# Rotary embedding over split heads on one core: the final wait for the stores moves from SyncE to GpSimd

## The chip, the core and the metric

The kernel runs on one core of a Trainium2 chip. The core has five engines, each with its own instruction stream: TensorE (PE), VectorE (DVE), ScalarE (ACT), GpSimd (POOL) and SyncE (SP); they meet only through semaphores. Bulk transfers are done by 16 DMA engines, which an engine starts by issuing a DMA instruction into its queue. The metric is device time in microseconds, lower is better. The kernel as it stands takes 161.19 us, the median of three runs (161.04 to 161.2).

## The reference: what is computed

`x` has 16 batches of 512 positions of 1024 float32 numbers, which are 16 heads of 64. Each head is cut into two halves of 32, and the two are rotated by a table of cosines and sines that depends on the position alone:

```python
x = x.reshape(batch, seq, num_heads, head_dim)
x1, x2 = x[..., :half_dim], x[..., half_dim:]
cos, sin = cos[None, :, None, :], sin[None, :, None, :]
rotated = np.concatenate([x1 * cos - x2 * sin, x1 * sin + x2 * cos], axis=-1)
```

The input and the output have 33.55 MB each, and every input element is read once and every output element is written once.

## The kernel before, in words

A **unit** is a 128 x 1024 tile: 128 partitions, one row of 16 heads in each. There are 64 units. Positions are spread over the partitions, four neighbouring rows per partition for a single batch (4 units, 2 MB, one DMA each way) or eight for a pair of batches (8 units, 4 MB, one DMA each way). The first two and the last two batches are handled as singles, the twelve between them as six pairs: ten loads and ten stores in all. The tiles live in `x_sb`, a ring of 40 units, and the result is written over the input in place.

The work of one unit is a product with the cosines, a product of the swapped halves with the signed sines, and their sum:

- POOL computes most of the sine products into `t2_sb` (`on_gpsimd`, line 263), in groups of one or two units. Its program begins with a memset and an `affine_select` that make the identity matrix, and it ends with the last product.
- DVE computes the cosine product into PSUM (line 302), a few of the sine products (line 295), and for two thirds of the units the sum (line 313).
- For the other third, PE adds `t2_sb` onto the cosine product in PSUM by a matmul with the identity (line 225), and ACT copies the sum back to `x_sb` (line 192).

ACT also issues every load (line 154) and the loads of the two tables (line 175). The six loads that fit into the ring are issued at the start; the last four wait until the store that frees their part of the ring has landed (semaphores `sem_out[k]`, of which there are `EARLY` = 3).

SP issues the stores and does nothing else (`on_sync`, lines 157 to 163). For each tile it waits until the last unit of the tile has been added up (`wait_added`, the waits at line 138), and issues the store (line 162). The first stores raise `sem_out[k]`, all later ones raise `sem_rest`; the six of `sem_rest` raise it by 16 each, to 96. The last instruction of SP's program is a wait for that 96 (line 163), so SP's program ends only when every store of these six has landed; the earlier stores are waited for by ACT ahead of the late loads. PE, ACT, POOL and DVE have no such last wait: their programs end with their last piece of arithmetic.

Of the kernel before, what the change touches and what calls it, by code (L numbers as in the profile page):

```python
# [6 lines left out]
def bass_split_heads_rope_kernel(  # L7
# [22 lines left out]
    R2 = 2 * R1  # L30
# [15 lines left out]
    NU = len(rows)  # L46
    EARLY = (NU - RING) // R2
# [24 lines left out]
    with ExitStack() as stack:  # L72
# [13 lines left out]
        sem_rest = stack.enter_context(nc.semaphore("rest"))  # L86
# [27 lines left out]
        def in_dram(single, pairs, t):  # L114
            b, n = tiles[t]
            return single[b] if n == R1 else pairs[:, b:b + 2, :]

        def in_sbuf(t):
            b, n = tiles[t]
            k = b * R1 % RING  # L120
            return x_sb[:, k:k + n].rearrange("p n h t d -> p (n h t d)")

        def where(u):
            t, r = rows[u]
            return t, r, u % RING
# [7 lines left out]
        def wait_added(eng, u):  # L133

            if n_pe[u]:
                eng.wait_ge(sem_a, n_pe[u])
            if n_comb[u]:
                eng.wait_ge(sem_v, n_comb[u])

        def wait_t2_free(eng, u):  # L140

            if u >= NT2:
                v = u - NT2
                if PE2[v]:
                    eng.wait_ge(sem_e, n_pe[v])
                else:
                    eng.wait_ge(sem_v, n_comb[v])

        def stores_of(k):

            return sum(b * R1 // R2 == k for b, _ in tiles)
# [4 lines left out]
        def on_sync(sp):  # L156
            for u in range(NU):
                t, r, k = where(u)
                if r == tiles[t][1] - 1:
                    wait_added(sp, u)  # L160
                    k = u // R2
                    sp.dma_start(in_dram(o1, o2, t), in_sbuf(t)).then_inc(sem_out[k] if k < EARLY else sem_rest, 16)
            sp.wait_ge(sem_rest, 16 * sum(stores_of(k) for k in range(EARLY, NU // R2)))

        def on_scalar(ae):
            later = {}
# [68 lines left out]
        def on_gpsimd(pl):  # L235
            pl.memset(ident[:], 1.0).then_inc(sem_i, 1)  # L236
            pl.wait_ge(sem_i, 1)
            pl.affine_select(  # L238
                out=ident[:],
                in_=ident[:],  # L240
                compare_op=mybir.AluOpType.is_equal,
                fill=0.0,
                base=0,
                pattern=[[-1, P]],
                channel_multiplier=1,
            ).then_inc(sem_i, 1)
            for u in range(NU):
                if V2[u] or (G2[u] and u % 2 == 1):
                    continue
                t, r, k = where(u)  # L250
                n = 2 if G2[u] else 1
                if (t, r) == (0, 0):
                    pl.wait_ge(sem_s, 1)
                if (t, r) == (2, 0):
                    pl.wait_ge(sem_s, 2)
                if r == 0:
                    pl.wait_ge(sem_in[t], 16)
                if n == 2 and u + 1 >= NT2:
                    pl.wait_ge(sem_m, u + 2 - NT2 + NT1)  # L259
                elif n == 1:  # L260
                    wait_t2_free(pl, u)
                table = (s1_sb if tiles[t][1] == R1 else s2_sb)[:, r:r + n]
                pl.tensor_tensor(  # L263
                    t2_sb[:, u % NT2:u % NT2 + n],
                    x_sb[:, k:k + n, :, ::-1, :],
                    table[:, :, None, :, :].broadcast_to([P, n, H, 2, HALF]),
                    mult,
                ).then_inc(sem_p, 1)

        def on_vector(ve):  # L270
            ve.memset(zero[:], 0.0).then_inc(sem_z, 1)  # L271
# [48 lines left out]
            for u in range(NU + LEAD):  # L320
                if u < NU:
                    mul(u)
                if u >= LEAD and not PE2[u - LEAD]:
                    comb(u - LEAD)

        on_sync(nc.sync)
        on_scalar(nc.scalar)
        on_gpsimd(nc.gpsimd)
        on_tensor(nc.tensor)
        on_vector(nc.vector)  # L330
# [33 lines left out]
```

## Time and profile before

| what | value |
|---|---|
| median of three runs | 161.19 us (161.04 to 161.2) |
| time of the profiled execution | 161.04 us |
| its span, first to last instruction of the program | 159.6 us |
| time outside the span | 1.4 us |
| busy: POOL, DVE, PE, ACT | 131.7, 129.6, 64.4, 24.3 us |
| moved by DMA | 67.25 MB, 421 GB/s over the span |
| last store: issued, landed | 151.9 us, 159.6 us |

The span begins with the first instruction of the program on any engine and ends with the last one. Instants in the text are microseconds from the span's start. An engine is called busy while it computes; semaphore waits and DMA issues are not counted. The letter q behind an engine's name means the part of it that issues instructions, its sequencer: SPq is where SP's waits and DMA issues are listed. Beside its instructions, the trace records when each semaphore was changed, also by instructions around the program that have no line of the kernel.

### The profile page before, as it was taken

The numbers are of one execution on the slowest core, as the hardware profiler recorded it, in microseconds if no ns is written. First come the engines' busy times: TensorE is split into PE (matmuls) and PEld (weight loads), VectorE is DVE, ScalarE is ACT, GpSimd is POOL, SyncE is SP. The second block draws the span as 40 slices with busy tenths as digits, with TensorE's granted clock in tenths as the row PEclk, the third lists the DMA queues.
The fourth block names the chain that finished last, engine by engine and source line by source line (L and its number), as shares of the span: only waits on it lengthen the run. The fifth ranks groups of instructions, "written<-read, shape, count | busy, mean of one in ns | idle before, by whom it ended". The sixth has DMA issues, their size and how long they took to land.

```text
span 159.6 us, 499 instructions
## 1 busy us (share of the span) xinstructions
PE 64.4 (40%) x94; PEld 22.2 (14%) x94; DVE 129.6 (81%) x117; ACT 24.3 (15%) x27; POOL 131.7 (82%) x41
## 2 busy tenths in 40 slices
PE   6050017076408870789067400575058506900000
PEld 1020011021102220222021100211021102300000
DVE  0069947999999989998999629999999999556900
ACT  0420002004300250023102040023202310220000
POOL 1069999999999999999999798992999999089400
PEclk9999999759985589557759985589957995585555
DMA  5999999999999999999999999999999999999997
GB/s 144 396 466 472 394 411 431 448 476 402 394 448 406 495 419 402 476 435 402 443 435 435 394 476 435 402 460 394 427 456 448 443 394 423 472 419 435 386 456 300
DMA packets 3169, 67.25 MB, mean 421 GB/s; under 512 B 352, under 2 KB 608, under 8 KB 608
## 3 DMA queue, kind: packets, MB, share of 16 engines
q10 hardware_dynamic: 1728, 33.69, 49.8%
q1 hardware_dynamic: 1440, 33.56, 48.9%
q14 instruction: 1, 0.01, 0.0%
HBM read 33.69 MB, written 33.55 MB: 421 GB/s over the span
## 4 chain that ended last, share of the span: by engine, by line
DMA 61%; DVE 17%; POOL 5%; PE 5%; issue 4%; ACTq 1%; ACT 1%; DVEq 0%; POOLq 0%; SPq 0%
DMA x_sb<-in_x_dram 43%; DMA out_dram<-x_sb 18%; DVE t_ps L302 8%; DVE x_sb L313 7%; POOL t_sb L263 5%; PE t_ps L225 5%; DVE t_sb L295 2%; ACT x_sb L192 1%; ACTq L154 1%; ACTq L175 1%; DVE tab_ps L280 0%; DVEq L312 0%; DVE tab_ps L281 0%; DVEq L299 0%; POOLq L259 0%
## 5 line engine op out<-in xcount | busy, mean ns | idle before, releaser
L263 POOL TENSOR_TENSOR t_sb<-x_sb,s_sb 128x2048 f32<-128x2048 f32 (+1 forms) x35 | 131.0, 3784 | 17.1 <-DMA x_sb<-in_x_dram 8.3
L225 PE MATMUL t_ps<-t_sb,ident 128*128 128x512 f32 x84 | 59.6, 857 | 69.1 <-DVE t_ps L302 56.7
L302 DVE TENSOR_TENSOR t_ps<-x_sb,pair_ps 128x1024 f32<-128x1024 f32 x48 | 57.5, 1221 | 5.2 <-ACT x_sb L192 5.2
L313 DVE TENSOR_TENSOR x_sb<-t_ps,t_sb 128x1024 f32<-128x1024 f32 x43 | 52.2, 1216 | 5.9 <-POOL t_sb L263 5.9
L192 ACT ACTIVATE x_sb<-t_ps 128x1024 f32<-128x1024 f32 x21 | 21.4, 1024 | 107.6 <-PE t_ps L225 99.9
L225 PEld LDWEIGHTS t_ps<-t_sb,ident 128*128 128x128 f32 x84 | 20.3, 267 | 108.2 <-DVE t_ps L302 78.7
L302 DVE TENSOR_TENSOR t_ps<-x_sb,tab_ps 128x1024 f32<-128x1024 f32 x16 | 19.2, 1222 | 2.6 <-DMA x_sb<-in_x_dram 2.5
L295 DVE TENSOR_TENSOR t_sb<-x_sb,tab_ps 128x1024 f32<-128x1024 f32 x6 | 7.3, 1209 | 0.0
L273 DVE COPY tab_ps<-stage 128x128 f32<-128x128 f32 x1 | 0.3, 296 | 7.6 <-DMA stage<-in_cos_dram 7.6
L209 PE MATMUL pair_ps<-stage,pick 128*128 128x256 f32 x4 | 2.0, 667 | 5.1 <-DMA stage<-in_sin_dram 5.1
L202 PE MATMUL t_ps<-zero 128*128 128x512 bf16 x6 | 2.7, 629 | 1.3 <-DVE zero L271 1.3
L178 ACT ACT_TABLE_LOAD x1 | 1.3, 1283 | 5.5 <-issue 5.5
L209 PEld LDWEIGHTS pair_ps<-stage,pick 128*128 128x128 f32 x4 | 1.2, 324 | 6.1 <-issue 6.0
L202 PEld LDWEIGHTS t_ps<-zero 128*128 128x128 bf16 x6 | 0.7, 136 | 2.4 <-DVE zero L271 1.2
L271 DVE MEMSET zero<- 128x256 uint32 x1 | 0.3, 272 | 0.9 <-PEq L346 0.9
L187 ACT ACTIVATE s_sb<-pair_ps 128x256 f32<-128x256 f32 x1 | 0.4, 384 | 1.7 <-PE pair_ps L209 1.7
L183 ACT ACTIVATE s_sb<-stage 128x128 f32<-128x128 f32 x1 | 0.3, 310 | 1.8 <-DMA stage<-in_sin_dram 1.8
L236 POOL MEMSET ident<- 128x128 f32 x1 | 0.2, 205 | 0.3 <-POOLq L346 0.3
L178 ACT ACTIVATE pick<-ident 128x256 f32<-128x256 f32 x1 | 0.4, 416 | 0.0
L188 ACT ACTIVATE s_sb<-pair_ps 128x256 f32<-128x256 f32 x1 | 0.4, 377 | 0.0
L238 POOL TENSOR_SCALAR_AFFINE_SELECT ident<-ident 128x128 f32<-128x128 f32 x1 | 0.3, 295 | 0.1
L346 POOL MEMSET const-float32-0.0<- 128x1 f32 x1 | 0.1, 99 | 0.3 <-issue 0.3
(6 smaller groups left out, 1.0 us busy)
## 6 DMA issues: line engine op xcount, KB each, us to landing
x_sb<-in_x_dram ACTq DMA_DIRECT2D x6, 4096.0 KB, 38.7
out_dram<-x_sb SPq DMA_DIRECT2D x6, 4096.0 KB, 25.3
x_sb<-in_x_dram ACTq DMA_DIRECT2D x4, 2048.0 KB, 22.7
out_dram<-x_sb SPq DMA_DIRECT2D x4, 2048.0 KB, 16.1
stage<-in_cos_dram ACTq DMA_DIRECT2D x1, 64.0 KB, 7.5
stage<-in_sin_dram ACTq DMA_DIRECT2D x1, 64.0 KB, 7.2
```

The source lines that it names most:

```text
L154: eng.dma_start(in_sbuf(t), in_dram(x1, x2, t)).then_inc(sem_in[t], 16)
L175: ae.dma_start(stage[:, i, :], table.rearrange("(s r) d -> s (r d)", r=R1)).then_inc(sem, 16)
L178: ae.activation(pick[:], ident[:].rearrange("q (s k) -> q k s", k=2)[:, :, :, None].broadcast_to([P, 2, P // 2, 2]), COPY).then_inc(sem_g, 1)
L187: ae.activation(s2[:, :, :, 0, :], pair_ps[:, :, 1, :, :], COPY, scale=-1.0)
L192: ae.activation(xs[:, u % RING, :], t1_ps[:, u % NT1, :], COPY).then_inc(sem_a, 1)
L202: pe.matmul(t1_ps[:, k, b * BANK:(b + 1) * BANK], zero[:, 0:P], zero[:], start=True, stop=True).then_inc(sem_w, 1)
L209: pe.matmul(pair_ps[:, k].rearrange("p c r d -> p (c r d)"), pick[:, k].rearrange("q s b -> q (s b)"), stage[:].rearrange("q c f -> q (c f)"),
L225: ins = pe.matmul(t1_ps[:, u % NT1, b * BANK:(b + 1) * BANK], ident[:], t2[:, b * BANK:(b + 1) * BANK], start=False, stop=True, skip_group ...
L263: pl.tensor_tensor(t2_sb[:, u % NT2:u % NT2 + n], x_sb[:, k:k + n, :, ::-1, :], table[:, :, None, :, :].broadcast_to([P, n, H, 2, HALF]), ...
L295: ve.tensor_tensor(t2_sb[:, u % NT2, :, :, :], swapped(k), over_heads(v_ps), mult)
L302: ve.tensor_tensor(t1_ps[:, u % NT1, :].rearrange("p (h d) -> p h d", d=HALF), x_sb[:, k, :, :, :].rearrange("p h t d -> p (h t) d"), c_of ...
L313: ve.tensor_tensor(xs[:, k, :], t1_ps[:, u % NT1, :], t2_sb[:, u % NT2, :, :, :].rearrange("p h t d -> p (h t d)"), add,).then_inc(sem_v, 1)
```

## The change

The last wait of SP's program is removed, and the same wait, for the same semaphore and the same value, is put behind the loop at the end of POOL's program. Nothing else is touched: the number of instructions, the DMAs and their order are the same.

```diff
@@ on_sync
                     sp.dma_start(in_dram(o1, o2, t), in_sbuf(t)).then_inc(sem_out[k] if k < EARLY else sem_rest, 16)
-            sp.wait_ge(sem_rest, 16 * sum(stores_of(k) for k in range(EARLY, NU // R2)))
@@ on_gpsimd
                     mult,
                 ).then_inc(sem_p, 1)
+            pl.wait_ge(sem_rest, 16 * sum(stores_of(k) for k in range(EARLY, NU // R2)))
```

## The prediction, made before the changed kernel was run

> **What bounds the kernel now.** I read the page first: the slices of the span, then the chain that ended last.
>
> ```profile
> span 159.6 us, 499 instructions
> ...
> DMA  5999999999999999999999999999999999999997
> ...
> DMA 61%; DVE 17%; POOL 5%; PE 5%; issue 4%; ACTq 1%; ACT 1%; DVEq 0%; POOLq 0%; SPq 0%
> ```
>
> The DMA engines are at 90% or more in 38 of 40 slices, and 61% of the chain is transfers. The kernel is bound by moving 67.25 MB; no engine's arithmetic can be what the change touches. Next, the end of the span: SP's waits, its last instruction, and the timeline of SP and POOL after 140 us.
>
> ```profile
> SPq L163 <- DMA out_dram<-x_sb: 7.4, 1, 7.4
> ```
> ```profile
> L163 SPq EVENT_SEMAPHORE  x1: 17/17/17, 159.6 to 159.6; - x1
> ```
> ```profile
> 140.88 11.33 SPq L162 DMA_DIRECT2D out_dram<-x_sb  x2
> ```
> ```profile
> 140.32 9.12 POOL L263 TENSOR_TENSOR t_sb<-x_sb,s_sb 128x2048 f32<-128x2048 f32 x3 [4.32 <-DMA x_sb<-in_x_dram]
> ```
>
> SP issues its last store by 140.88 + 11.33 = 152.2 us and waits 7.4 us for it; this wait is the last instruction of the whole program. POOL's last product ends at 140.32 + 9.12 = 149.44, so POOL stands still for 10.2 us before the same landing. The landing doesn't depend on who waits: whatever the change does, it does in the 1.4 us between the span (159.6) and the time (161.04).
>
> What happens there has no row in the views, but the trace's record of semaphore updates goes on past the span. One semaphore, number 2, belongs to none of the program's instructions. It is raised nine times in a burst, twice ahead of the first instruction and twice at the end (us from the span's start):
>
> ```
> ahead 1: -7.857 -3.493 -2.871 -2.827 -2.804 -2.691 -2.653 -2.619 -2.569
> ahead 2: -0.371 -0.336 -0.298 -0.254 -0.231 -0.120 -0.081 -0.047 -0.001
> end 1:  139.968 140.968 149.973 151.952 159.739 159.783 159.822 159.856 159.904
> end 2:  160.868 160.902 160.940 160.984 161.008 161.106 161.144 161.178 161.225
> ```
>
> The first five of "end 1" fit the ends of the five engines, read from the last update that each made: PE 139.812, ACT 140.868, POOL 149.450, DVE 151.813, and SP's wait that ends at 159.629. So I read it as a barrier that walks a fixed chain, PE, ACT, POOL, DVE, SP, and then back, DVE, POOL, ACT, PE; an engine raises the count when its predecessor has. Between the two end barriers about 240 other semaphores change once each, from 159.864 to 160.472, in five blocks of neighbouring numbers; the last block (3 to 53, ending 160.472) starts after PE's release at 159.904. Then "end 2" starts, with PE. So from PE's release everything follows in a fixed 161.225 - 159.904 = 1.32 us.
>
> **The change, step by step.**
>
> *Removed: SP's wait.* SP's program ends at 152.2. Its end then lies under the store's 7.4 us and costs nothing; SP stands in the chain behind DVE, which arrives at 151.952, and would have to wait for POOL anyway. What leaves the path is SP's arrival, 159.739 - 159.629 = 0.110 us, and the way back from SP, 159.904 - 159.739 = 0.165 us. Together 0.275 us.
>
> *Added: POOL's wait.* Nothing in the program is queued behind it: it stands after POOL's last product, no DMA is issued by POOL, and no engine waits for POOL's wait. What is behind it is POOL's place in the barrier, and DVE and SP, which follow in the chain, now wait for POOL. The instruction itself is the same (17 ns on SPq; the program's opening wait on POOLq is 17 ns too):
>
> ```profile
> L346 POOLq EVENT_SEMAPHORE  x2: 17/17/17, 0.6 to 0.7; - x2
> ...
> L346 SPq DRAIN  x1: 7/7/7, 0.0 to 0.0; - x1
> ...
> L346 POOLq DRAIN  x1: 187/187/187, 0.4 to 0.4; - x1
> ```
>
> How quickly POOL notices a landing: its product at 140.32 starts 0.068 us after the last update of that load (140.252), DVE's at 140.28 0.028 us after. I take 0 more than SP and keep 0.05 for the range.
>
> *The way through the barrier with POOL last.* DVE and SP must still go up, then four steps back. The other bursts show just that, from the third update to the ninth: 161.225 - 160.940 = 0.285, -0.001 + 0.298 = 0.297, -2.569 + 2.871 = 0.302 us; in "ahead 1" POOL really was the late one, by 0.62 us. Mean 0.295 against SP's 0.165: **+0.13 us**. The steps aren't alike: SP to DVE takes 0.044 where DVE had long been waiting, and 0.098 to 0.113 where DVE itself had just gone up, as it would here.
>
> The Trainium skill, "Runtime: NRT & Kernel Launch", section on the preamble and postamble, describes such a pass over five engines with 44 ns a step and about 355 ns for eight. "End 2" takes 0.357 us for its eight steps, so the total agrees; by equal steps, POOL last would have six steps to go where SP has four, +0.09 us, an estimate. That would put the sum 0.04 lower than by the rows.
>
> *POOL's own arrival.* This is the disputed term. From an engine's last update to its raise of semaphore 2: PE 0.156, ACT 0.100, DVE 0.139, SP 0.110, but POOL 149.973 - 149.450 = **0.523 us**. Today that is hidden: DVE is 2 us later, SP 10 us. After the change it stands in the open. Below, it can't be much less than the other engines' 0.100. Above, all 0.523 stays, and something may be added: POOL's sequencer was free from about 147.1, when its last product started, so closing instructions of POOL that ran under that 2.35 us product would come into the open too. The nearest rows for such are POOL's opening ones (MOVE 35 ns, INC_SWDGE_SEM 27 ns), so I bound it at 0.2.
>
> Which part is tied to finishing arithmetic? In the opening, POOL's DRAIN reports at 0.625 (update of semaphore 96), 0.12 after the last memset (0.40 + 0.10), where idle engines' DRAINs take 7 to 10 ns. So I let 0 to 0.12 of the 0.523 fall away when POOL has been idle for 10 us, and 0.40 to 0.52 stay. I take 0.47, which is 0.36 more than SP's 0.110.
>
> *Sum:* 0.13 + 0.36 = **+0.49 us** on the profiled execution: 161.04 + 0.49 = 161.53. The bounds are 0.13 - 0.01 = +0.12 and 0.13 + 0.41 + 0.2 + 0.05 = +0.79. The profiled execution was the lowest of the three runs, 0.15 below the median; the runs differ by their transfers, not by this end, so against the median I predict 161.19 + 0.49 = **161.68 us**. This kernel's measurement can tell 0.2% or 0.32 us from no change, so "slower" begins at 161.51.
>
> **The rivals.**
>
> *A: POOL's 0.523 us is only the tail of its product.* Then a POOL that has idled arrives like the others (0.100 to 0.156), and only the barrier's +0.13 is left: 161.32, not slower by what can be told. For it: POOL's spans are the least exact of the page, and only one arrival of POOL after arithmetic is in the trace. Against it: consecutive products follow without a gap (three in 9.12 us: 4.50 + 2.35 + 2.35 and a little overlap), so a finished product leaves no 0.4 us behind, and the DRAIN row allows 0.12. It decides if POOL arrives less than 0.30 us after its wait ends.
>
> *B: the time doesn't contain the barrier.* If the 1.4 us lay ahead of the first instruction, the end would be the last wait on either engine: 161.19, at most 0.05 more. Against it: the last update is 161.225 - 159.629 = 1.60 us after SP's wait, and the 1.41 us fit inside that but for 0.19.
>
> *C: SP's ending is what costs.* SP's stores are its queue's; if SP's closing has to settle that queue, it would now be done under the 7.4 us, and the barrier might close sooner. The most that leaves the path is the 0.275 us above, and POOL must arrive and return in no time: 160.92. SP's arrival of 0.110 beside ACT's 0.100 shows nothing heavy.
>
> *D: POOL's hidden closing is long.* The 2.35 us product could cover more than my 0.2; then 161.98 and up, without a row for it.
>
> **How the numbers follow.** Forecast (+0.33 to +0.79): 0.60. D: 0.06. A: 0.24. B: 0.07. C: 0.03. The forecast and D are slower, 0.66; A and B within 0.2%, 0.31; C, to which I leave the chance of a real gain, faster, 0.03. The range goes from 161.2, which takes in A and half of B, to 162.0, the upper bound 161.19 + 0.79; outside are C, most of D and half of B, with run-to-run differences of 0.1 about 0.15 in all.
>
> **What would show it.** In the changed profile the span should stay within the transfers' own differences of 159.6, its last instruction an EVENT_SEMAPHORE on POOLq in place of SPq, after an idle stretch of about 10 us on POOL. The loads, stores and products should show the same durations. The third update of semaphore 2 should be the late one, about 0.47 us after POOL's wait (A: 0.10 to 0.16); DVE and SP should follow in 0.044 and 0.024, and the ninth update 0.295 after the third. From there to the end it should be 1.32 us as now. I'm wrong if the time outside the span stays at 1.4 us (A would make it 1.5, the forecast 1.9), or if a store's issue or landing moved by more than the runs differ, for which I see no reason.

## The result, and the profile after

The changed kernel takes 162.0 us, the median of eight runs (161.69 to 162.9), against 161.19 us of the kernel before (eight runs, 161.04 to 161.58). The ratio is 1.0046, with a 95% interval of 1.0028 to 1.0065: slower by about half a per cent. The profiled execution took 161.95 us with a span of 160.0 us. In the experiments below, a few executions, of the kernel before too, took 3 to 7 us longer than the rest, and all ratios, medians and counts leave these out.

The page's head, slices and chain of the changed kernel:

```profile
span 160.0 us, 499 instructions
...
DMA  5999999999999999999999999999999999999997
...
DMA 61%; DVE 17%; POOL 5%; PE 5%; issue 4%; ACTq 1%; ACT 1%; DVEq 0%; POOLq 0%; SPq 0%
```

This is the old picture: nothing in the body has another bound. What changed is the last instruction. First POOL's wait (the row of line 268), then SP's last stores in the timeline, then POOL's last products:

```profile
L268 POOLq EVENT_SEMAPHORE  x1: 17/17/17, 160.0 to 160.0; - x1
```
```profile
142.32 10.18 SPq L162 DMA_DIRECT2D out_dram<-x_sb  x2
```
```profile
140.60 9.12 POOL L262 TENSOR_TENSOR t_sb<-x_sb,s_sb 128x2048 f32<-128x2048 f32 x3 [4.54 <-DMA x_sb<-in_x_dram]
```

SP's program ends at 142.32 + 10.18 = 152.5 us by this row. POOL is done with its arithmetic at 149.72, and its wait of 17 ns is now the last instruction of the program. The product's line numbers are one lower, since a line went away above them.

The updates of semaphore 2, the barrier around the program, at the end of the two profiled executions (us from the span's start; the span ends at 159.629 before and at 159.976 after):

```
before, end 1: 139.968 140.968 149.973 151.952 159.739 159.783 159.822 159.856 159.904
before, end 2: 160.868 160.902 160.940 160.984 161.008 161.106 161.144 161.178 161.225
after,  end 1: 141.409 142.406 160.513 160.556 160.580 160.676 160.715 160.749 160.796
after,  end 2: 161.761 161.796 161.834 161.877 161.901 162.000 162.038 162.072 162.119
```

Before, the fifth raise (SP) is the late one; after, it is the third (POOL), and DVE and SP follow it at once. **POOL's arrival** is 160.513 - 159.976 = 0.537 us after its wait ends, where SP's was 0.110. **The way** from the late raise to PE's release, the ninth raise, is 0.283 us, where SP's was 0.165. From PE's release to the last raise are 1.323 us, before 1.321. So the time outside the span went from 161.04 - 159.63 = 1.41 us to 161.95 - 159.98 = 1.97 us, +0.56, and 0.43 + 0.12 of it are these two terms.

The rest of the difference of the medians, 0.81 - 0.56 = 0.25 us, is in the span: in all eight runs the time exceeds the span by 1.94 to 2.00 us, so what they have beyond that is span. It isn't explained by either term and is followed up below.

### The profile page after: what moved, and what is told of

It is laid out like the page before. It is cut to its first block, busy times and chain, and to the rows that moved or that the text cites. A ratio compares the mean times of both kernels' runs of the same rounds, so it can differ in the third digit from the quotient of the medians.

```text
span 160.0 us, 499 instructions
## 1 busy us (share of the span) xinstructions
PE 69.5 (43%) x94; PEld 24.0 (15%) x94; DVE 129.7 (81%) x117; ACT 24.3 (15%) x27; POOL 131.6 (82%) x41
## 4 chain that ended last, share of the span: by engine, by line
DMA 61%; DVE 17%; POOL 5%; PE 5%; issue 4%; ACTq 1%; ACT 1%; DVEq 0%; POOLq 0%; SPq 0%
DMA x_sb<-in_x_dram 42%; DMA out_dram<-x_sb 18%; DVE t_ps L302 8%; DVE x_sb L313 7%; POOL t_sb L262 5%; PE t_ps L224 5%; DVE t_sb L295 2%; ACT x_sb L191 1%; ACTq L154 1%; ACTq L174 1%; DVE tab_ps L280 0%; DVEq L312 0%; DVE tab_ps L281 0%; DVEq L299 0%; POOLq L258 0%
## 5 line engine op out<-in xcount | busy, mean ns | idle before, releaser
L224 PE MATMUL t_ps<-t_sb,ident 128*128 128x512 f32 x84 | 64.7, 929 | 65.3 <-DVE t_ps L302 53.0
L224 PEld LDWEIGHTS t_ps<-t_sb,ident 128*128 128x128 f32 x84 | 22.1, 291 | 107.8 <-DVE t_ps L302 76.6
```

The lines of the kernel that those rows point to most:

```text
L224: ins = pe.matmul(t1_ps[:, u % NT1, b * BANK:(b + 1) * BANK], ident[:], t2[:, b * BANK:(b + 1) * BANK], start=False, stop=True, skip_group ...
```

## The experiments

All ratios are to the kernel before, run on the same chip in turn. The table gathers what the profiled executions show; the columns "arrival" (from the end of the last wait or instruction to the raise of semaphore 2 by that engine) and "way" (from there to the ninth raise) are read from the record of updates.

| kernel | last to arrive | time | span | outside | arrival | way | ratio (95% interval) |
|---|---|---|---|---|---|---|---|
| again_before | SP | 161.49 | 160.07 | 1.42 | 0.110 | 0.163 | 1.0002 (0.9993 to 1.0011) |
| sp_twice | SP | 161.26 | 159.85 | 1.41 | 0.110 | 0.165 | 1.0007 (0.9998 to 1.0016) |
| wait_dve | DVE | 161.39 | 159.86 | 1.53 | 0.146 | 0.242 | 1.0015 (1.0001 to 1.0029) |
| wait_act | ACT | 161.60 | 160.01 | 1.59 | 0.119 | 0.324 | 1.0001 (0.9982 to 1.0021) |
| wait_pe | PE | 162.81 | 159.74 | 3.07 | 0.187 | 0.355 | 1.0062 (1.0034 to 1.0091) |
| again_after | POOL | 162.32 | 160.35 | 1.97 | 0.537 | 0.286 | 1.0062 (1.0045 to 1.008) |
| third_after | POOL | 161.74 | 159.78 | 1.97 | 0.537 | 0.286 | 1.0053 (1.004 to 1.0066) |
| wait_both | POOL | 161.75 | 159.80 | 1.96 | 0.537 | 0.285 | 1.0032 (1.0022 to 1.0043) |
| wait_both_2 | POOL | 161.78 | 159.81 | 1.97 | 0.537 | 0.286 | 1.0032 (1.002 to 1.0045) |
| after_sp_pad | POOL | 162.10 | 160.13 | 1.97 | 0.538 | 0.282 | 1.0046 (1.0033 to 1.0059) |
| pool_memset | POOL | 162.09 | 160.15 | 1.94 | 0.517 | 0.285 | 1.005 (1.0038 to 1.0062) |
| sp_155 | POOL | 161.72 | 159.76 | 1.97 | 0.538 | 0.286 | 1.0049 (1.0031 to 1.0066) |

**The theory and its rivals.** Theory 1 is the prediction's: each engine has its own closing, and its place in the chain sets how many steps are left. Rivals: the place is nothing and POOL's closing is all; or it isn't POOL at all but SP, whose program now ends while its stores are under way.

**The two kernels again, as a control and for the spans.** No edit.

> The kernel before, unchanged, as a control. Theory 1 (the added time is all outside the span: 0.53 us of POOL's own closing plus 0.28 us of way through the chain, against SP's 0.11 and 0.165): time minus span 1.41 us, ratio 1.000. It also gives the spans of before, of which only one, 159.6, was shown; the rival to be told apart is that the change lengthens the span too, by about 0.25 us (half of what was measured over the forecast).

> The changed kernel, unchanged, on the same chip as the control. Theory 1: time minus span 1.97 us, and a median span within 0.1 us of the control's, so a ratio of 1.0034 (0.56 of 161.2). Rival (the span is lengthened by the change as well): median span 0.25 us or more above the control's, ratio 1.005.

The control is the kernel before to 1.0002, and its 1.42 us outside the span is the old 1.41. The changed kernel has 1.97 again, and a ratio whose interval lies above 1.0034: the span is longer as well (median 160.3 us, the control's 159.9). The head of the control's page, then that of the changed kernel's:

```profile
span 160.1 us, 499 instructions
```
```profile
span 160.3 us, 499 instructions
```

**Both engines wait.** It tells POOL's part from SP's.

```diff
 # on top of the changed kernel, at the end of on_sync
+            sp.wait_ge(sem_rest, 16 * sum(stores_of(k) for k in range(EARLY, NU // R2)))
```

> POOL's wait as in the changed kernel, and SP keeps its own. Theory 1 (POOL's place and POOL's closing): as the changed kernel, time minus span 1.97 us, third update of semaphore 2 about 0.53 us after the wait, ratio 1.0034. Rival (what costs is that SP's program ends while its stores are under way): as before, time minus span 1.41 us, ratio 1.000; and if that is what lengthened the span, the span is as the control's.

```profile
SPq L163 <- DMA out_dram<-x_sb: 7.4, 1, 7.4
```
```profile
L269 POOLq EVENT_SEMAPHORE  x1: 17/17/17, 159.8 to 159.8; - x1
```

SP waits its 7.4 us as before the change, and the end still costs 1.96 us outside the span: the cost outside is POOL's and not that of SP's early end. But the ratio is 1.0032, as these 0.55 us alone would make it: the longer span isn't there (median 159.8 us).

**The wait on DVE, on ACT, on PE.** SP's wait is removed and put behind the last instruction of the other engine's program:

```diff
+            ve.wait_ge(sem_rest, ...)     # wait_dve, end of on_vector
+            ae.wait_ge(sem_rest, ...)     # wait_act, end of on_scalar
+            pe.wait_ge(sem_rest, ...)     # wait_pe,  end of on_tensor
```

> The wait stands at the end of DVE's program, and nowhere else. Theory 1: DVE arrives 0.12 to 0.14 us after its wait, then 0.024 up to SP and 0.098 + 0.038 + 0.034 + 0.047 back: 0.36 to 0.38 us from the end of the wait to PE's release against SP's 0.275, so time minus span 1.50 to 1.52 us, ratio 1.0006. Rival (any engine but SP costs as much as POOL, since SP has gone ahead): 1.97 us, ratio 1.0034.

> The wait stands at the end of ACT's program alone, second in the chain. Theory 1 (own closing plus way): ACT arrives 0.10 to 0.13 us after its wait, and from ACT's raise to the end of the chain are 0.32 us; 0.43 us against SP's 0.275, time minus span 1.56 to 1.58 us, ratio 1.001. Rival (the place in the chain is nothing, an engine's closing is all): 1.41 us, ratio 1.000.

> The wait stands at the end of PE's program alone, at the head of the chain. Theory 1: PE arrives about 0.16 us after its wait and the whole chain follows, 0.357 us: 0.51 us to PE's release against SP's 0.275, time minus span 1.65 us, ratio 1.0015 from the end alone. Rival (POOL's closing is all that costs, the place in the chain is nothing): 1.41 to 1.46 us. SP ends early here too: if that lengthens the span, the median is 0.25 us more.

The last instruction of each, in the order DVE, ACT, PE:

```profile
L324 DVEq EVENT_SEMAPHORE  x1: 21/21/21, 159.8 to 159.8; - x1
```
```profile
L196 ACTq EVENT_SEMAPHORE  x1: 17/17/17, 160.0 to 160.0; - x1
```
```profile
L233 PEldq EVENT_SEMAPHORE  x1: 51/51/51, 159.7 to 159.7; - x1
```

The raises of semaphore 2 around the release, in the same order:

```
wait_dve, end 1: 141.145 142.144 150.179 160.002 160.025 160.123 160.161 160.197 160.244
wait_act, end 1: 140.602 160.131 160.169 160.213 160.237 160.334 160.372 160.408 160.455
wait_pe,  end 1: 159.922 159.956 159.994 160.038 160.061 160.158 160.196 160.230 160.277
```

These show the chain with each engine as the late one. DVE: only the fourth raise is late; ACT: the second; PE: all nine come after its wait. The ways are 0.242, 0.324 and 0.355 us, with POOL's 0.285 and SP's 0.165 in between by their places. So the order PE, ACT, POOL, DVE, SP is shown, and the place does cost. The arrivals of SP, ACT, DVE and PE are 0.110, 0.119, 0.146 and 0.187 us; POOL's 0.537 is the odd one. Outside the span DVE has 1.53 and ACT 1.59 (expected 1.50 to 1.52 and 1.56 to 1.58). In ratios ACT's 0.18 us and DVE's 0.12 are hardly to be told from none, as expected.

PE missed its expected 1.65. The barrier itself behaves (0.187 + 0.355 us), and the second one begins 0.51 us after the last of the changes between the two, where it is 0.40 before the change; its last raise is at 161.70. That would make about 161.5. The time is 162.81. The runs fall into two groups, five of 161.52 to 161.77 and five of 162.81 to 163.56; the lower group is what the chain makes (about 1.8 us outside the span), the upper has 1.2 us more that no update shows. The trace is one of the upper group, and its DMA record holds a packet that none of the other thirteen traces has: 16 KB on queue 8, of the kind "instruction", starting at 161.82 us, 0.12 us after the last raise, and taking 1.29 us. That is about the missing time. No run of the lower group was kept as a trace, so that this packet makes the difference between the groups is not shown.

**What is in POOL's 0.537 us.** One more instruction behind the wait:

```diff
             pl.wait_ge(sem_rest, ...)
+            pl.memset(ident[:], 1.0)
```

> The changed kernel with one more POOL instruction behind the wait, a memset of the identity matrix (0.2 us; it is no longer needed by then). If POOL's 0.53 us is a fixed closing that follows its last instruction of any kind, POOL's raise of semaphore 2 comes 0.50 to 0.55 us after the memset ends, 0.75 to 0.85 us after the wait. If a POOL that has idled must first be woken and this is most of the 0.53, the memset itself starts late and the raise follows its end in 0.1 to 0.2 us.

POOL's timeline of this kernel, start and duration in us:

```profile
159.94 0.20 POOL L269 MEMSET ident<- 128x128 f32 x1 [10.25 <-DMA out_dram<-x_sb]
```

The memset starts 0.05 us after the landing (the last update of the stores is at 159.894), so POOL isn't slow to wake after 10 us of rest. POOL's raise is 0.517 us after the memset's end. After a product, before the change, it was 0.523; after a bare wait 0.537. So it is a closing of fixed length that follows whatever comes last. What POOL does in it has no row; that only POOL has it is shown, why is not.

**The longer span.** Five runs were to find it.

> The changed kernel a third time. Outside the span 1.97 us in any case. If the 0.25 us beyond that belongs to this program, the median is again 0.7 us or more over the kernel before (ratio 1.0045 or more); if it was a matter of which runs were drawn, the ratio is 1.0034.

```diff
 # after_sp_pad: on top of the changed kernel, at the start of on_sync
+            sp.wait_ge(sem_cos, 16)
```

> The changed kernel, and SP begins with a wait for the cosines (there at 8.5 us, 11 us before the first store), so that SP's program has as many instructions as before but still ends at 152 us. Theory 1: outside the span 1.97 us, ratio at least 1.0034. If the lengthened span comes from SP's program being one instruction shorter, the span is as the control's (ratio 1.0034, runs close together as with both waits). If it comes from SP's early end, it stays (1.0045 or more, runs spread over 0.5 us or more).

> Waits on POOL and SP a second time. Outside the span 1.97 us. If SP's remaining wait is what keeps the span short, the median is again 0.45 to 0.55 us above the kernel before (161.75) and the runs lie close together; if the eight runs of the first time were luck, the median is 0.7 us or more above it, as the changed kernel's.

```diff
 # sp_twice: on top of the kernel before, at the end of on_sync
             sp.wait_ge(sem_rest, ...)
+            sp.wait_ge(sem_rest, ...)
```

> The kernel before with SP's last wait written twice: an edit that should cost one wait that is already met (0.02 to 0.05 us), as a measure of what any edit of a program does to the span. If an edit as such shifts the span by 0.25 us, it shows here as a ratio of 1.0015 or more; otherwise 1.0002.

```diff
 # sp_155: on top of the changed kernel; sem_last is new
-   .then_inc(sem_out[k] if k < EARLY else sem_rest, 16)
+   .then_inc(sem_out[k] if k < EARLY else sem_last if t == NT - 1 else sem_rest, 16)
+            sp.wait_ge(sem_rest, 80)          # end of on_sync
-            pl.wait_ge(sem_rest, 96)          # written as a sum in the kernel
+            pl.wait_ge(sem_rest, 80)
+            pl.wait_ge(sem_last, 16)
```

> The changed kernel, with the last store on a semaphore of its own, so that SP can wait at its end for the five stores before it (met at about 155 us), while POOL waits for those five and then for the last one. Outside the span 1.97 us in any case. If the 0.3 us that the changed kernel's span is longer belong to SP ending at 152 us, before its stores have landed, the median span is as the control's and the time about 0.5 us above the kernel before, its runs close together; if SP has to stay to the very end, or if it is something else in the program, the time is about 0.85 us above it. Since the lag of the slowest DMA engine is there by 150 us in the profiles, I expect SP's stay between 152 and 155 us to change nothing.

The effect came again: 1.0053 in the third trial of the changed kernel, with its interval clear of the 1.0035 that 0.56 us make, and 1.0046 with SP's program as long as before (median span 160.1 us; the interval begins at 1.0033, so this run alone doesn't settle it). The 1.005 with the memset is no third case: the memset itself ends 0.25 us after the landing where the bare wait ends 0.04 after it, and 0.53 us outside the span with these 0.21 make 1.0046. It stayed away a second time with both waits (161.69 to 161.99, ratio 1.0032). An edit as such doesn't make it: the doubled wait has 1.0007, with 1 in its interval. Nor does SP's early end by itself: with the wait on DVE, ACT or PE, SP's program ends at 152 us too, and the median span is 159.8 us in all three, like that of the kernel before run beside them, where the three trials of the changed kernel have 160.05, 160.3 and 160.2. With SP at 155 us the eight runs go from 161.72 to 163.03, four within 161.72 to 161.78 like those of both waits, four above; this decides nothing.

Where the span grows can be read from the landings. In all fourteen traces, from the landing of the third store from the end (at about 150 us) to that of the last are 9.65 to 9.72 us. What differs is there by 150 us: that landing is at 149.92 in the first profile, and at 150.59 in again_after, the longest span. Most of it is there by 141 us: the store before that landed at 140.44 and 140.91. In the last store the first of the 16 DMA engines reports at 158.8 to 159.1 in every profile, and the last one anywhere from 159.6 to 160.3: the span ends with the slowest engine's lag, and that lag is older (first to last report of the third store from the end: 149.13 to 149.92 in the first profile, 149.22 to 150.59 in again_after). SP's program ends at 152 us, and POOL comes to its wait at 149.7, so neither can have made what was there at 141. That the longer span came in all three trials of the changed kernel, where POOL waits alone, and was absent in both trials where SP waits beside POOL, is measured; **the cause is not settled**.

## Why the prediction was right

- *The landing doesn't depend on who waits, the change acts outside the span.* Right for two thirds of the difference: 0.56 of 0.81 us. The other 0.25 us were in the span, for which the prediction saw no reason beyond the runs' own differences. This is the step that failed, and it nearly cost the range: the median 162.0 is its upper end. That it stayed inside is luck: in the two later trials of the changed kernel the medians are 162.3 and 162.2, which is 1.04 and 0.95 us above the kernel before run beside them.
- *Nothing is queued behind POOL's wait, SP's early end costs nothing.* Right outside the span: with SP's wait kept beside POOL's, the end costs the same 1.96 us. SP's early end by itself doesn't lengthen the span either (DVE, ACT, PE); whether SP's wait does something for the span where POOL waits stays open, though the lag is older than either wait.
- *The way through the barrier, +0.13.* Measured 0.282 to 0.286 against SP's 0.165, +0.12. The three bursts already in the trace of before were a good measure, and the chain's order, read from five arrivals, holds for every engine that was put last. In its account of the other semaphores the last block begins at number 7, not 3 (numbers 3 to 6 have no update), which changes no term.
- *POOL's arrival, 0.47, which is 0.36 more than SP's.* Measured 0.537, 0.43 more. The mis-sized part is the 0 to 0.12 us that were let fall away after a rest. Nothing fell away: the closing is as long after a rest as after a product or a memset.
- *Sum +0.49.* Outside the span +0.56, from the mechanism that was forecast; with the span +0.81.
- *Rival A, POOL's tail,* is refuted by the memset and by the 0.537. *Rival B, the time doesn't contain the barrier,* is refuted: the last raise of semaphore 2 and the time keep a distance of 0.17 to 0.19 us in every profile but that of wait_pe, with spans that differ by 0.7 us. *Rival C, SP's ending costs,* is refuted: SP arrives in 0.110, the shortest of the arrivals after a last wait, and with SP's wait kept or gone the end costs the same 1.96 to 1.97 us. *Rival D, a longer hidden closing of POOL:* 0.537 against 0.523 leaves 0.014 us for it.

## What to carry to other kernels

Here the last thing the program does is to wait for its stores: every engine's program ends early but that of the one which waits, and that engine's closing and its place in the closing barrier are paid in full. In these runs SP is the cheapest (0.275 us from the end of the wait to the release), then DVE (0.39), ACT (0.44), PE (0.54, and in half of its runs 1.2 us more) and POOL (0.82). By these numbers such a wait belongs on SP. Look at the updates behind the last instruction when a time changes and the span doesn't. When a forecast of half a microsecond is met by 0.8, look at the span of several runs before adding a story to the mechanism.

## What the runs showed of the hardware that was not expected

- POOL raises the barrier's semaphore 0.52 to 0.54 us after its last instruction, whatever that is; the other four engines 0.10 to 0.19 us.
- The steps of the barrier differ: 0.034 (PE to ACT), 0.038, 0.044, 0.024 (DVE to SP), and back 0.098 or 0.044 (SP to DVE, shorter when DVE has long been waiting), 0.038, 0.034, 0.047.
- With the last wait on PE, half of the runs took 1.2 us more than the barrier's updates account for; the one trace of such a run has an instruction packet of 16 KB and 1.29 us behind the last raise. The second barrier began 0.11 us later. Why either happens is not shown.
- The 16 DMA engines end a stream of 67 MB up to 1.4 us apart (158.95 to 160.31 in again_after), so a span can move by some tenths of a microsecond with the same program and the same bytes.
